# A matmul with a decayed cumulative sum: two PSUM banks for each of the first four tiles, weights loaded slot by slot, finer first pieces, and a last store in halves of time

## Chip, cores and metric

One core of one Trainium2 chip. The metric is the device time of the whole kernel in microseconds (us); several executions were timed and medians are quoted. The profiled execution has a span some 2 us shorter than its time, because the span begins with the first instruction.

## The reference

```python
# x (16, 2048, 1024), w (1024, 1024), decay (1024,), all float32
xw = x @ w
out[:, 0, :] = xw[:, 0, :]
for t in range(1, S):
    out[:, t, :] = decay[None, :] * out[:, t - 1, :] + xw[:, t, :]
```

## The kernel before

The 32768 rows of x are 64 chunks of 512 times. A **slot** is one output tile of 128 channels for a pair of chunks (1024 times, two PSUM banks, 16 matmuls), and the last two chunks make slots of one chunk each. For each chunk GpSimd issues loads that cast x to bf16, VectorE turns 32x32 blocks ("turn"), and ScalarE sorts the result into `xt` ("part"). TensorE leaves channels on partitions and time along the row. Then either VectorE scans PSUM directly, or, for "paired" tiles, ScalarE copies and scales (`pair`), GpSimd adds even to odd times, VectorE scans half as many elements with the squared decay, and GpSimd fills in the rest. VectorE turns the tile back, SyncE stores it. Every engine works in the order of a hand-written agenda.

```python
dec2 = psp.tile([128, 512], FP32, name="dec2")        # squared decay, has a PSUM bank to itself
...
def load_w(queue, h, e, m0=0, m1=M):                  # h: half of the columns, e: even/odd row, m: block
    for q in range(NQ):                               # four transfers of 32 partitions
        pin(queue.dma_start(
            out=stage[h, e, m0][quad(q)].rearrange("p (m d) -> p m d", m=m1 - m0),
            in_=_ap(w, [[2 * D, P], [2 * P * D, m1 - m0], [1, CH]],
                    (q * CQ + m0 * 2 * P + e) * D + h * CH)))
...
for _ in range(34):                                   # warming matmuls on zeros
    pin(nc.tensor.matmul(out=spare, lhsT=idle[:, 0:128], rhs=idle, start=True, stop=True))
load_w(nc.sync, 0, 0, 0, M // 2)                      # the others go out on GpSimd's queue
...
agenda = {                                            # M/L: x loads, U: w loads, W/w: w copy on VectorE/ScalarE,
    -99: "M0 M1 U0 U1 M2 M3 U2 U3 L L L W0 w1 E0 F0 G0 w3 W2 E1 F1 G1 W4 w5 W6 w7 E2 F2 D G2 E3 F3 G3 W8 W9 W10 W11",
    0: "w12 L L w13 P0 S0",                           # E/T: turn, F/G/X/Y: part, P: pair, S: scan,
    1: "w14 L P1 L",                                  # C: complete, B: turn back and store
    2: "S1 W15 P2 B0 S2",
    3: "T2 L S3 C0 C1 C2",
    4: "L P4 X2 L Y2 L B2 T3 B1 L",
    ...
    -1: "B-3 P-1 S-1 B-2 C-5 B-1 C-1 C-2",
}
...
heads = [ring(psp, "ps", 3, [128, T]) for _ in range(3)]     # three tiles with both banks
firsts = [ps[:, 0:TL] for ps in heads] + [spare]             # the fourth has one bank
# chunk 0 for four tiles, chunk 1 for three; the fourth's second half takes
# a bank of "ps" that the first scan has to free
...
for k in range(K):                                           # every later slot
    for l, c in enumerate(g):
        matmul(ps[:, l * TL:(l + 1) * TL], n, k, xt_of[c])
```

## Time and profile before

| | before |
|---|---|
| median of three executions | 915.26 us (915.03 to 915.39) |
| profiled span | 912.5 us |
| TensorE's first real matmul, from the start of the span | 11.20 us |
| TensorE's last matmul ends | 901.58 us |
| from there to the end (the "tail") | 10.9 us |

TensorE's work is fixed at 884 us, so only the beginning, the tail and waits between can be shortened. The prediction below shows the lines of the page, the timeline, the chain and the windows that say so. How to read them: in a timeline the first number is the start, the second the length, the brackets hold the idle time ahead and who ended it. In the chain of waits the first number is when a piece began and the second how long it lasted; for a DMA that is from issue to landing.

### The profile page before, as it was taken

Reading aid. Unit: us, or ns where it says so; the run is one execution under the profiler, and the core shown is the slowest. Engines: PE = TensorE matmul, PEld = TensorE weight load, DVE = VectorE, ACT = ScalarE, POOL = GpSimd, SP = SyncE. Lnnn points to the kernel's source line nnn. Section 1 sums busy time; section 2 is a strip of 40 time slices with the busy share of each in tenths; the row PEclk is TensorE's granted clock in tenths of the full one; section 3 lists DMA queues with packets and bytes.
Section 4 is the critical chain, followed back from the end, with each engine's and each line's share of the span. In section 5 each row is a group of like instructions: output and inputs, shape, how many; then the busy total and the mean of one; then the engine's idle time right before and its main releaser. Section 6 shows DMA issues by size and latency. Waiting matters only on the chain.

```text
span 912.5 us, 11926 instructions
## 1 busy us (share of the span) xinstructions
PE 891.3 (98%) x4088; PEld 408.5 (45%) x4170; DVE 826.0 (91%) x613; ACT 685.8 (75%) x950; POOL 664.4 (73%) x764
## 2 busy tenths in 40 slices
PE   8899999999999999999999999999999999999995
PEld 4444444444444444444444444444444444444442
DVE  4999999999999999999999999999999999999986
ACT  3778887877877777778778778778778778777753
POOL 8688878777777777777677777777787776776552
PEclk9999999999999999999999999999999999999998
DMA  9999999999999999999999999999999999999668
GB/s 170 166 220 215 215 230 235 256 250 255 247 237 255 247 237 224 230 233 231 223 235 227 224 231 229 230 226 231 227 224 230 231 230 224 232 229 207 151 151 219
DMA packets 406253, 204.49 MB, mean 224 GB/s; under 512 B 12976, under 2 KB 405936, under 8 KB 406192
## 3 DMA queue, kind: packets, MB, share of 16 engines
q1 hardware_dynamic: 268848, 134.76, 59.5%
q0 software_dynamic: 137344, 68.96, 56.8%
q8 instruction: 32, 0.52, 0.2%
q14 instruction: 29, 0.24, 0.1%
HBM read 138.42 MB, written 134.22 MB: 299 GB/s over the span
## 4 chain that ended last, share of the span: by engine, by line
PE 90%; DMA 3%; POOL 2%; issue 2%; DVE 2%; ACT 1%; SPq 0%; DVEq 0%; POOLq 0%
PE ps L126 90%; DMA xb<-in_x_dram 2%; POOL xb L105 1%; DMA ot<-in_w_dram 1%; DVE so L194 1%; DVE xw L115 1%; POOL ot L245 1%; PE spare L126 0%; DMA out_dram<-ot 0%; DVE so L180 0%; POOL so L208 0%; ACT xt L123 0%; DVE ot L215 0%; POOL xs L174 0%; ACT xs L168 0%
## 5 line engine op out<-in xcount | busy, mean ns | idle before, releaser
L126 PE MATMUL ps<-xt,wsb 128*128 128x512 bf16 (+1 forms) x4011 | 874.2, 377 | 9.0 <-DVE so L194 2.6
L126 PEld LDWEIGHTS <-wsb 128*128 128x128 bf16 x4136 | 404.6, 98 | 485.7 <-issue 5.6
L174 POOL TENSOR_TENSOR xs<-h,xs 128x512 f32<-128x512 f32 (+1 forms) x193 | 245.3, 1271 | 195.5 <-ACT h L158 88.3
L168 ACT COPY xs<-ps 128x1024 f32<-128x1024 f32 (+1 forms) x193 | 191.6, 993 | 158.8 <-PE ps L126 149.3
L215 DVE STREAM_TRANSPOSE ot<-so 128x1024 f32<-128x1024 f32 (+1 forms) x264 | 302.7, 1184 | 1.9 <-POOL so L208 1.1
L208 POOL TENSOR_TENSOR so<-h,xs 128x512 f32<-128x512 f32 (+1 forms) x193 | 244.3, 1266 | 34.5 <-ACT h L158 18.1
L123 ACT COPY xt<-xw 128x2048 bf16<-128x2048 bf16 (+1 forms) x128 | 239.8, 1875 | 7.5 <-DVE xw L115 7.5
L105 POOL DMA_DIRECT2D xb<-in_x_dram x264 | 174.1, 660 | 2.0 <-POOLq L435 0.9
L158 ACT ACTIVATE h<-so,dec 128x512 f32<-128x512 f32 (+1 forms) x193 | 147.1, 763 | 36.0 <-DVE so L180 32.1
L115 DVE STREAM_TRANSPOSE xw<-xb 128x2048 f32<-128x2048 f32 (+1 forms) x66 | 146.7, 2222 | 6.1 <-DMA xb<-in_x_dram 6.1
L180 DVE TENSOR_TENSOR_SCAN so<-dec,keep,xs 128x512 f32<-128x512 f32 (+1 forms) x99 | 121.6, 1229 | 29.8 <-POOL xs L174 29.6
L180 DVE TENSOR_TENSOR_SCAN so<-dec,xs 128x512 f32<-128x512 f32 x94 | 114.8, 1222 | 31.3 <-POOL xs L174 28.2
L158 ACT ACTIVATE h<-ps,dec 128x512 f32<-128x512 f32 (+1 forms) x193 | 131.8, 683 | 0.0
L194 DVE TENSOR_TENSOR_SCAN so<-dec,ps 128x1024 f32<-128x1024 f32 x33 | 74.5, 2261 | 0.0
L194 DVE TENSOR_TENSOR_SCAN so<-dec,keep,ps 128x1024 f32<-128x1024 f32 (+1 forms) x33 | 73.4, 2225 | 0.0
L211 ACT COPY keep<-so 128x1 f32<-128x1 f32 x136 | 25.1, 187 | 0.3 <-DVE so L194 0.3
L173 ACT COPY so<-keep 128x1 f32<-128x1 f32 x99 | 19.0, 192 | 0.7 <-DVE ot L215 0.7
L171 POOL MEMSET so<- 128x1 f32 x94 | 11.0, 117 | 3.2 <-DVE ot L215 3.2
L262 PE MATMUL spare<-idle 128*128 128x512 bf16 x34 | 10.2, 473 | 1.2 <-DVE idle L259 1.2
L126 PE MATMUL spare<-xt,wsb 128*128 128x512 bf16 (+1 forms) x43 | 11.2, 359 | 0.1
L245 POOL DMA_DIRECT2D ot<-in_w_dram x16 | 9.0, 561 | 2.4 <-issue 0.7
L253 ACT COPY wsb<-ot 128x512 bf16<-128x512 bf16 x6 | 3.4, 615 | 5.7 <-DMA ot<-in_w_dram 5.7
(18 smaller groups left out, 20.3 us busy)
## 6 DMA issues: line engine op xcount, KB each, us to landing
out_dram<-ot SPq DMA_DIRECT2D x248, 512.0 KB, 10.6
xb<-in_x_dram POOLq DMA_DIRECT2D x248, 256.0 KB, 7.8
out_dram<-ot SPq DMA_DIRECT2D x12, 256.0 KB, 4.2
xb<-in_x_dram POOLq DMA_DIRECT2D x16, 128.0 KB, 5.0
ot<-in_w_dram POOLq DMA_DIRECT2D x12, 128.0 KB, 5.2
out_dram<-ot SPq DMA_DIRECT2D x8, 128.0 KB, 2.8
ot<-in_w_dram SPq DMA_DIRECT2D x4, 128.0 KB, 3.5
ot<-in_w_dram POOLq DMA_DIRECT2D x4, 64.0 KB, 4.3
```

Of the source, the lines that this page charges most:

```text
L105: pin(nc.gpsimd.dma_start(out=xb_of[c][quad(q), j0:j1], in_=_ap(x, [[D, P], [P * D, j1 - j0], [1, CQ]], (b * S + t0 + j0 * P) * D + q * CQ)))
L115: pin(nc.vector.transpose(out=dst.rearrange("p (m j i) -> p j m i", m=M, i=P)[:, j0:j1], in_=src.rearrange("p (j m c) -> p j m c", m=M, c=P)))
L123: pin(copy(out=xt_of[c][:, m0:m1, :, j0 * P:j1 * P], in_=src))
L126: pin(nc.tensor.matmul(out=ps[:, t0:t1], lhsT=wsb[:, k, n].rearrange("p q i -> p (q i)"), rhs=xt[:, k // 2, k % 2, t0:t1], start=(k == 0 a ...
L158: pin(nc.scalar.activation(out=h, in_=src, func=mybir.ActivationFunctionType.Copy, scale=dec[:, self.n:self.n + 1]))
L168: pin(nc.scalar.copy(out=self.xs, in_=self.ps))
L174: pin(nc.gpsimd.tensor_tensor(out=self.xs[:, 1:T:2], in0=g, in1=self.xs[:, 1:T:2], op=ALU.add))
L180: pin(nc.vector.tensor_tensor_scan(out=so[:, 3:T + 2:2], data0=dec2[:, n:n + 1].to_broadcast([128, T // 2]), data1=self.xs[:, 1:T:2], init ...
L194: pin(nc.vector.tensor_tensor_scan(out=so[:, t:t + size], data0=dec[:, n:n + 1].to_broadcast([128, size]), data1=ps, initial=before, op0=A ...
L208: pin(nc.gpsimd.tensor_tensor(out=so[:, 2:T + 2:2], in0=h, in1=self.xs[:, 0:T:2], op=ALU.add))
L211: pin(nc.scalar.copy(out=self.keep, in_=so[:, T + 1:T + 2]))
L215: pin(nc.vector.transpose(out=self.ot[:, :, n % R * P:(n % R + 1) * P], in_=self.so[:, 2:T + 2].rearrange("p (i t) -> p i t", t=P)))
```

## The change

The intent: the squared decay gives up its PSUM bank, so that all four first tiles have two banks and none waits for a scan. Each weight transfer now holds one (half, parity, block) for all 128 partitions, so that each copy needs one landing instead of four, in the order in which they are used. The first turns and parts are cut finer and the warming is shorter, so that real work can start earlier. At the end the last two tiles are turned and stored in two halves of time.

```diff
-    dec2 = psp.tile([128, 512], FP32, name="dec2")
+    squares = [const.tile([128, K], FP32, name="squares")]   # a PSUM bank after slot 7 ("d")
...
-    def load_w(queue, h, e, m0=0, m1=M):
-        for q in range(NQ):
-            pin(queue.dma_start(
-                out=stage[h, e, m0][quad(q)].rearrange("p (m d) -> p m d", m=m1 - m0),
-                in_=_ap(w, [[2 * D, P], [2 * P * D, m1 - m0], [1, CH]],
-                        (q * CQ + m0 * 2 * P + e) * D + h * CH)))
+    def load_w(queue, i):
+        h, e, m = i // 8, i // 4 % 2, i % 4
+        m0 = M // 2 if (h, e) == (0, 0) and m >= M // 2 else 0
+        pin(queue.dma_start(
+            out=stage[h, e, m0][:, (m - m0) * CH:(m - m0 + 1) * CH],
+            in_=_ap(w, [[CQ * D, NQ], [2 * D, P], [1, CH]], (m * 2 * P + e) * D + h * CH)))
...
+    pin(nc.scalar.copy(out=idle[:, 0:1], in_=idle[:, 1:2]))  # the warming has to wait for it
-    for _ in range(34):
+    for _ in range(27):
...
-    load_w(nc.sync, 0, 0, 0, M // 2)
+    load_w(nc.sync, 0)
+    load_w(nc.sync, 1)
...
-        -99: "M0 M1 U0 U1 M2 M3 U2 U3 L L L W0 w1 E0 F0 G0 w3 W2 E1 F1 G1 ...
-        0: "w12 L L w13 P0 S0",
-        1: "w14 L P1 L",
-        2: "S1 W15 P2 B0 S2",
+        -99: "M0 M1 U2 U3 U4 U5 U6 U7 M2 M3 U8 ... U13 w1 U14 L U15 W0 L L L E0 F0 G1 E1 L F2 G3 ...
+        0: "L P0",
+        1: "w13 w14 S0",
+        2: "L P1 P2 S1 L S2 w12 B0",
... (slots 3 to 16 sorted anew)
-        -1: "B-3 P-1 S-1 B-2 C-5 B-1 C-1 C-2",
+        -1: "B-3 P-1 S-1 a-2 C-5 a-1 C-1 C-2 b-2 b-1",     # a, b: first and second half of time
...
-            firsts = [ps[:, 0:TL] for ps in heads] + [spare]
+            firsts = [ps[:, 0:TL] for ps in heads] + [spares[0]]
+            seconds = [ps[:, TL:T] for ps in heads] + [spares[1]]
...
+        if left == 2 - R:                                      # buffers of the last two tiles
+            outlets = [Outlet(range(n, K), nj // 2, i) for i in range(2)]
...
+            if step == K:                                      # slot 8: all of its first chunk, then the second
+                todo.sort(key=lambda kl: kl[1])
```

## The prediction

> **What bounds the kernel now.** I read the page first (busy shares), then the timeline of TensorE, then the chain that ended last, then the windows of the last 30 us. The page says which engine, the timeline says where that engine is not at work.
>
> ```profile
> span 912.5 us, 11926 instructions
> PE 891.3 (98%) x4088; PEld 408.5 (45%) x4170; DVE 826.0 (91%) x613; ACT 685.8 (75%) x950; POOL 664.4 (73%) x764
> ...
> L126 PE MATMUL ps<-xt,wsb 128*128 128x512 bf16 (+1 forms) x4011 | 874.2, 377 | 9.0 <-DVE so L194 2.6
> ```
>
> TensorE is busy for 98% of the span. The work is fixed: 32768 rows are 64 chunks of 512, each chunk takes 8 output tiles x 8 contractions, so 4096 matmuls of 512 columns, before and after. The 377 ns is the pipelined length of one, not its rate; the rate comes from the timeline, where the long pieces of the chain repeat every 10.79 us for 50 matmuls, 0.2158 us each. 4096 x 0.2158 = 884 us. So at most 912.5 - 884 = 28.5 us of the span is open to any change that leaves the matmuls alone. Where it lies:
>
> ```profile
> 1.20 10.17 PE L262 MATMUL spare<-idle 128*128 128x512 bf16 x34 [1.20 <-DVE idle L259]
> 11.20 0.49 PE L126 MATMUL ps<-xt,wsb 128*128 128x256 bf16 x3
> ...
> 13.01 0.50 PE L126 MATMUL ps<-xt,wsb 128*128 128x256 bf16 x3 [0.77 <-DVE wsb L253]
> ...
> 14.89 0.49 PE L126 MATMUL ps<-xt,wsb 128*128 128x256 bf16 x3 [0.83 <-DVE xt L123]
> ...
> 20.64 5.70 PE L126 MATMUL ps<-xt,wsb 128*128 128x256 bf16 x48 [0.39 <-DVE xt L123]
> 27.59 1.89 PE L126 MATMUL ps<-xt,wsb 128*128 128x512 bf16 x7 [1.25 <-DVE so L194]
> 29.77 7.07 PE L126 MATMUL ps<-xt,wsb 128*128 128x512 bf16 x32 [0.29 <-DVE so L194]
> 37.69 27.79 PE L126 MATMUL ps<-xt,wsb 128*128 128x512 bf16 x125 [0.86 <-DVE so L194]
> 65.71 4.48 PE L126 MATMUL ps<-xt,wsb 128*128 128x512 bf16 x20 [0.23 <-DVE so L194]
> ```
>
> First number: start; second: length; in brackets the idle time before and who ended it. Real work starts at 11.20, right behind 34 warming matmuls on zeros. By 37.69 the first six slots (96 matmuls, 20.7 us) are done: 37.69 - 11.20 - 20.7 = 5.8 us idle, in two kinds: early on it waits for weights and input pieces, from 26 to 38 us for a scan to free a PSUM bank. From 37.69 on 4000 matmuls x 0.2158 = 863.2 us would end at 900.9; they end at 901.6. So the middle is full. The tail from 901.6 to 912.5 is 10.9 us. Sum: 11.2 + 5.8 + 0.7 + 10.9 = 28.6.
>
> ```profile
> 24.38 8.03 DMA xb<-in_x_dram
> ...
> 38.70 2.28 DVE xw L115
> ...
> 42.81 1.89 ACT xt L123
> ```
>
> In the chain, the beginning is loads: the issue and landing times in the trace show the transfers landing in order, 256 KB of source every 0.65 us (about 400 GB/s), with never more than eight in flight. Chunk 3 has landed at 37.8, is turned until 41.0 and copied until 44.7, and slot 8, the first that needs it, starts at about 44.6.
>
> ```profile
> 902.00:903.00 1.00, 0.00 (x0) 0.00 (x0) 1.00 (x2) 0.00 (x0) 0.26 (x1) 1.00 0.94 238
> ...
> 908.00:909.00 1.00, 0.00 (x0) 0.00 (x0) 0.00 (x0) 0.00 (x0) 0.00 (x0) 0.50 0.92 198
> ```
>
> After TensorE's last matmul the windows show the DMA engines at 0.92 to 0.94 (last but one column) up to 911. The queue of stores has been without a gap since 895: the last twelve issues follow each other at 0.6 to 1.1 us, the last at 908.66 lands at 911.30. VectorE's last transpose is done at 905.55, 3 us before that issue. The tail is stores that drain, not VectorE.
>
> **What the Trainium skill says.** "TensorE: Matmul & The Clock Gate", section "Wait — 56ns, not 53.3ns?", gives 215.7 ns from start to start for 512 columns warm; the trace has 215.8, so the floor stands. "PSUM — Partial Sum Buffer", section "Terms", says that one matmul output is at most one bank of eight: before, three pairs of banks plus one spare bank plus one bank that only held the squared decay; head 3 of the beginning had no second bank, and its second half had to wait for a scan, which is the 1.25 us wait above. "DMA: Bandwidth & Descriptors", section "Why a DMA increments its semaphore by 16 and not by 1", says that a transfer spreads over the largest number up to 16 that divides the slowest dimensions of both sides. The old weight loads have 32 on both sides, so 16 engines; the new ones have 128 in the buffer and 4 in memory, so 4 engines. No transfer of that form is in this trace; this is my main risk. The same page, section "Rules for kernel authors", says that under 64 KB one pays mostly overhead; the new half stores are 64 KB each.
>
> **The change part by part.**
> Warming: 27 instead of 34 matmuls, 7 x 0.213 = 1.5 us less; they end at about 9.7.
>
> First piece: x half 0 landed at 8.48. Before, a turn of 1.25 and a copy of 1.05 stood before the first matmul. VectorE's turns of 1024 and 2048 elements took 1.25 and 2.29, so a quarter of 512 takes about 0.21 + 0.52 = 0.73; a copy of one m 0.37 on VectorE and 0.62 on ScalarE (by the same line through 1.05 and 1.90). So 8.60 + 0.73 + 0.37 = 9.7, and TensorE starts at 9.8: **1.4 us earlier**.
>
> Weights by slot: the same 4 MB in 16 transfers instead of 20, each usable alone. With one landing per 0.65 us after 11.20, the six transfers for the first half land from 11.9 to 15.3, x of chunk 1 from 15.9 to 20.5 (before 16.2 to 21.2), the second half of w until 27.1, chunk 2 until 31.1, chunk 3 until 36.4 (before 37.8).
>
> Four heads: TensorE then does chunk 0 by 19.0 (20.3 before; the wait for half 1 of x at 11.2 stays, 1.8 us), starts chunk 1 at 19.2 and finishes all four heads at about 26.3, instead of three at 26.3 and the fourth at 29.3. Slot 4 takes the banks of head 0, free when VectorE's first scan ends: VectorE has copied its last weights at 24.4, the scan takes 2.27, 26.65. Then a new wait: the weight piece for slot 4's second contraction is copied on ScalarE behind slot 2's two copies (25.7 + 0.9 + 0.7 + 0.6), ready at 27.9. So slot 4 runs from about 27.9 less two matmuls, 2.3 us earlier than 29.77, and then four slots x 3.45 bring slot 8 to **41.4** against 44.6.
>
> Slot 8: chunk 3 landed at 36.4; VectorE reaches its turn at 38.0 (scans, one turn, three transposes queued before it), done 40.2; ScalarE has two tiles' copies first, so the two pieces are ready at 42.5 and 44.3. The change sorts slot 8 by chunk, so they are needed at 43.1 and 44.0: a wait of 0.3. After it: slot 10 wants the scan of slot 7 (VectorE free at 48.0, TensorE there at 48.6), slot 11 wants ScalarE's copies of slot 8 (51.6 against 52.0). Close, both met. So 3.0 us remain gained when the full stretch begins, and its 0.2 and 0.2 us of waits before 65.7 stay.
>
> Squares: a tiny multiplication, once in SBUF and once into the freed bank; 0.17 us on VectorE, nothing.
>
> Tail: VectorE's two last transposes become four of half the length, the first half's data is complete some 0.5 us sooner. But the store queue is then still issuing older stores. Four issues of 128 KB at 0.62 become eight of 64 KB; at the same bytes per us 8 x 0.31, at the 0.25 to 0.38 of the smallest issues in the trace (the decay loads) up to 8 x 0.35. The second halves go into a buffer whose stores must have landed first (before: 906.55), later than VectorE is ready, but no later than the queue is. Net 0, with 0.4 either way.
>
> Sum: 1.4 (start) + 1.6 (fewer idle us until slot 8) = 3.0, less 0.3 for a quarter to a third of a risk that the new weight loads cost 1 us: 2.8. 915.26 - 2.8 = **912.4**.
>
> **Rivals.**
> (a) The weight loads run on four engines each. The first two, from the sync queue, would both sit on the same four and make the x pieces late there; w pieces would land near 6 and 9 instead of 6.5 at the latest, x half 0 after 9.5. For it: the page's rule and the shape. Against it: consecutive transfers may rotate over engines, and the author cut the warming to 27, which fits a start at 9.7. It would cost 1 to 1.5 us at the start and some of the later landings: 913.5 to 915.
> (b) The gain at the beginning is given back because VectorE, nearly without idle time from 25 to 65 us in the trace, has the same work to do in less time, and a scan holds up slot 10 to 14 (as the wait of 0.23 at 65.71 shows already). For it: total VectorE work rises slightly (quarters have fixed costs). Against it: the order of the transposes is changed so that scans come first. It would leave 1 to 1.5 us: 914.
> (c) The loads bind less than I think and slot 8 can start at 40: 911. Against it: landings at 400 GB/s.
> (d) The tail gains because the last piece is smaller, or loses by issue cost: 0.5 us either way.
>
> **Range and chances.** 909.8 to 915.0 covers (a) to (d) singly and half of (c) with (d); the runs before spread by 0.36. Faster by over 2% would take 18.3 us of the 28.5 that are open, while start and tail keep some 20: 1%. Slower by over 2% needs a new standing wait in the middle, whose code is unchanged: 1%.
>
> **What would show it.** TensorE's first real matmul at 9.8 (not 11.2); no wait for a scan of 1.25 us before the last head; slot 4 near 27.5 and slot 8 near 41.4; TensorE idle 4 us instead of 5.8 before that, some of it before slot 4 on a weight copy; then full to the end near 898.6; a tail of 10.9 us with the DMA engines above 0.9. The prediction fails if the weight transfers land later than the pieces before, or if waits for scans of over 1 us appear between 45 and 70 us.

## The result, and the profile after

**The kernel became slower: 925.51 us (925.00 to 926.06, five executions) against 915.26 (913.81 to 915.55, five executions).** The ratio is 1.0115, with a 95% interval of 1.010 to 1.013. Ratios here and below are the mean time of one kernel's runs over that of the other's of the same rounds, so not quite the ratio of the medians. The chances favoured "within 2%", which came true, but 925.5 lies far outside the range of 909.8 to 915.0, and the sign was wrong.

The page after, the same three lines as before:

```profile
span 923.5 us, 11920 instructions
...
PE 894.2 (97%) x4081; PEld 408.6 (44%) x4163; DVE 829.2 (90%) x623; ACT 687.4 (74%) x956; POOL 665.6 (72%) x762
...
L126 PE MATMUL ps<-xt,wsb 128*128 128x512 bf16 (+1 forms) x3996 | 877.0, 379 | 15.4 <-DVE xt L123 6.2
```

Waits ahead of the matmuls grew from 9.0 to 15.4 us, the largest part is for input (`xt`). Where they lie, in TensorE's timeline of the first 75 us:

```profile
2.29 8.04 PE L275 MATMUL spare<-idle 128*128 128x512 bf16 x27 [2.29 <-ACT idle L273]
15.04 0.80 PE L126 MATMUL ps<-xt,wsb 128*128 128x256 bf16 x3 [4.71 <-DVE xt L123]
...
19.84 1.44 PE L126 MATMUL ps<-xt,wsb 128*128 128x512 bf16 x3 [0.70 <-DVE xt L123]
...
31.29 2.34 PE L126 MATMUL ps<-xt,wsb 128*128 128x256 bf16 x20 [0.38 <-DVE xt L123]
...
36.39 0.38 PE L126 MATMUL ps<-xt,wsb 128*128 128x512 bf16 x1 [1.88 <-DVE so L194]
39.88 35.41 PE L126 MATMUL ps<-xt,wsb 128*128 128x512 bf16 x150 [3.11 <-ACT wsb L265]
```

Warming ends at 10.3 and real work starts at 15.04, not at the predicted 9.8. Three matmuls of 256 columns take 0.80 us where they took 0.49 before: the clock is at half speed. Slot 4 loses 1.88 us to a scan and 3.11 us to the copy of a weight piece, and starts in earnest at 39.88 instead of 29.77. From there TensorE is full. It ends at 912.07, 10.5 us later than before, and the tail is 11.4 us, 0.5 longer: 10.5 + 0.5 = 11.0, the difference of the spans.

What the first matmul waited for is in the chain:

```profile
2.60 10.91 DMA xb<-in_x_dram
...
15.23 7.18 DMA ot<-in_w_dram
...
27.33 9.34 DMA ot<-in_w_dram
36.69 1.14 ACT wsb L265 x2
...
39.32 0.52 ACT wsb L265
```

The third piece of x, issued at 2.60 as before, took 10.9 us to land; before, issued at the same moment, it took 5.2. The code of the x loads is unchanged. From 15 us on the chain is weights, which TensorE finally waits for at 39.88. The windows from 12 to 18 us, before and then after, show the same (the last two columns are the DMA engines' mean share and GB/s, the one before them the clock):

```profile
12.00:18.00 6.00, 4.35 (x33) 3.02 (x32) 2.67 (x5) 2.80 (x4) 5.78 (x11) 1.00 1.30 186
```

```profile
12.00:18.00 6.00, 2.60 (x12) 1.67 (x12) 3.30 (x6) 2.47 (x4) 4.85 (x7) 0.61 0.70 85
```

Loads move at 85 instead of 186 GB/s, and the sixteen DMA engines are busy half as much on the mean (this share adds up packets that overlap, so it can exceed 1), while transfers are outstanding. The queue of DMA issues lists the median from issue to landing: 5.0 us for the first x pieces before, 6.7 after, and 5.2 against 7.1 for the weights of 128 KB.

| landed at, us | before | after |
|---|---|---|
| chunk 0, first half | 8.48 | 13.69 |
| last weight piece | 27.07 | 38.97 |
| chunk 3 (slot 8 needs it) | 37.77 | 48.22 |

Everything that the beginning needs comes 5 to 12 us later. In the tail, the windows show stores still draining, as before:

```profile
915.00:920.00 5.00, 0.00 (x0) 0.00 (x0) 1.28 (x4) 0.00 (x0) 0.00 (x0) 0.50 0.98 201
```

### The profile page after: what moved, and what is told of

The parts are those of the page before. It is cut to its first block, busy times and chain, and to the rows that moved or that the text cites. A ratio compares the mean times of both kernels' runs of the same rounds, so it can differ in the third digit from the quotient of the medians.

```text
span 923.5 us, 11920 instructions
## 1 busy us (share of the span) xinstructions
PE 894.2 (97%) x4081; PEld 408.6 (44%) x4163; DVE 829.2 (90%) x623; ACT 687.4 (74%) x956; POOL 665.6 (72%) x762
## 4 chain that ended last, share of the span: by engine, by line
PE 93%; DMA 3%; POOL 1%; issue 1%; ACT 0%; DVE 0%; SPq 0%; DVEq 0%; POOLq 0%
PE ps L126 93%; DMA ot<-in_w_dram 2%; DMA xb<-in_x_dram 1%; POOL ot L258 1%; DMA out_dram<-ot 0%; PE spare L126 0%; POOL xb L105 0%; DVE ot L219 0%; SPq L240 0%; ACT wsb L265 0%; ACT xs L167 0%; DVE so L194 0%; ACT h L157 0%; DVE so L179 0%; POOL xs L173 0%
## 5 line engine op out<-in xcount | busy, mean ns | idle before, releaser
L126 PE MATMUL ps<-xt,wsb 128*128 128x512 bf16 (+1 forms) x3996 | 877.0, 379 | 15.4 <-DVE xt L123 6.2
L219 DVE STREAM_TRANSPOSE ot<-so 128x1024 f32<-128x1024 f32 (+2 forms) x266 | 302.7, 1176 | 2.0 <-issue 1.2
L179 DVE TENSOR_TENSOR_SCAN so<-spare,keep,xs 128x512 f32<-128x512 f32 (+1 forms) x99 | 121.7, 1230 | 30.5 <-POOL xs L173 30.2
L179 DVE TENSOR_TENSOR_SCAN so<-spare,xs 128x512 f32<-128x512 f32 x90 | 110.0, 1222 | 30.7 <-POOL xs L173 27.7
L126 PE MATMUL spare<-xt,wsb 128*128 128x512 bf16 (+1 forms) x58 | 14.3, 361 | 0.2 <-issue 0.2
L170 POOL MEMSET so<- 128x1 f32 x94 | 10.9, 116 | 0.4 <-DVE ot L219 0.4
L275 PE MATMUL spare<-idle 128*128 128x512 bf16 x27 | 8.0, 470 | 2.3 <-ACT idle L273 2.3
```

Of the source, the lines that this page charges most:

```text
L126: pin(nc.tensor.matmul(out=ps[:, t0:t1], lhsT=wsb[:, k, n].rearrange("p q i -> p (q i)"), rhs=xt[:, k // 2, k % 2, t0:t1], start=(k == 0 a ...
L179: pin(nc.vector.tensor_tensor_scan(out=so[:, 3:T + 2:2], data0=squares[-1][:, n:n + 1].to_broadcast([128, T // 2]), data1=self.xs[:, 1:T:2 ...
L219: pin(nc.vector.transpose(out=outlet.ot[:, :, c0:c0 + P], in_=self.so[:, 2 + t0:2 + t0 + nj * P].rearrange("p (i t) -> p i t", t=P)))
```

## The experiments

The theory after the result (A): the new weight transfers are slow because of their shape, they hold up the x loads as well, and nearly the whole loss is theirs. Rivals: (B) the new order of work on ScalarE and VectorE, above all the weight copy put behind two pairs; (C) TensorE's clock, cold after a long wait; (D) the tail; (E) the squared decay in SBUF. Twelve kernels were run. "Before" is the kernel before on the same chip and in the same rounds, whose medians were 914.85 to 915.27.

**1. The change with the old weight loads.** Only `load_w` and its calls go back; heads, order, parts, squares and tail stay.

```diff
-        "U": lambda i: load_w(nc.gpsimd, i),
+        "U": lambda i: load_w(nc.gpsimd, *{2: (0, 0, M // 2, M), 4: (0, 1), 8: (1, 0), 12: (1, 1)}[i]),
-        -99: "M0 M1 U2 U3 U4 U5 U6 U7 M2 M3 U8 U9 U10 U11 U12 U13 w1 U14 L U15 ...
+        -99: "M0 M1 U2 U4 M2 M3 U8 U12 w1 L ...        # and load_w as before
```

> The changed kernel with the weight loads of the kernel before (20 transfers with 32 as the slowest dimension on both sides), everything else as changed. Theory A (the cause is the shape of the new weight loads, which run on few DMA engines): x half 0 lands near 8.5 us again, the first real matmul is at 9.8 to 10.3, no cold stretch of the clock before the end, slot 4 at 27 to 29; time 911 to 914.5. Rival B (the quarters, the new order of the copies and the banks are at fault): first matmul after 12, a wait of some 3 us before slot 4's second contraction stays, time 920 or more.

Measured: 916.38 us (914.42 to 918.00), ratio 1.0011 (0.9995 to 1.0027), no difference clear of noise to before. Chunk 0's half landed at 8.66, the last weight at 27.74, chunk 3 at 38.45. The profiled execution was the slowest of the four (918.0). Its timeline:

```profile
10.16 0.49 PE L126 MATMUL ps<-xt,wsb 128*128 128x256 bf16 x3
...
25.25 0.60 PE L126 MATMUL ps<-xt,wsb 128*128 128x256 bf16 x4 [1.54 <-DVE xt L123]
26.33 3.89 PE L126 MATMUL ps<-xt,wsb 128*128 128x256 bf16 x20 [0.48 <-DVE xt L123]
...
32.42 24.06 PE L126 MATMUL ps<-xt,wsb 128*128 128x512 bf16 x108 [0.99 <-ACT wsb L265]
```

So 925.51 - 916.38 = 9.1 us of the loss go with the old loads, and TensorE starts at 10.16. But the 2.8 us that I had expected to gain do not come either: this version is level with the kernel before.

**2. The kernel before with the new weight loads.** The converse.

```diff
-    load_w(nc.sync, 0, 0, 0, M // 2)
+    load_w(nc.sync, 0)
+    load_w(nc.sync, 1)
-        load_w(nc.gpsimd, *((0, 0, M // 2, M), (0, 1), (1, 0), (1, 1))[i])
+        for s in ((2, 3), (4, 5, 6, 7), (8, 9, 10, 11), (12, 13, 14, 15))[i]:
+            load_w(nc.gpsimd, s)                        # and load_w as after
```

> The kernel before with only the weight loads replaced by the new ones (one transfer for each slot, 128 partitions against 4 as the slowest dimension in memory). Theory A: x half 0 lands at 12 to 14 us, first real matmul after 14, the last weight piece after 36, time 921 to 926. Rival B: within 1 us of the kernel before.

Measured: 926.23 us (925.48 to 927.05), ratio 1.0122 (1.0106 to 1.0139), as slow as the whole change. Chunk 0's half landed at 13.40, the last weight at 37.47, chunk 3 at 48.31. In its timeline the first real work and the wait that comes last are

```profile
15.55 0.80 PE L126 MATMUL ps<-xt,wsb 128*128 128x256 bf16 x3 [4.09 <-DVE xt L123]
...
47.79 12.39 PE L126 MATMUL ps<-xt,wsb 128*128 128x512 bf16 x48 [2.48 <-DVE so L194]
```

The loads alone reproduce the loss. It doesn't need the new order (B), nor the tail (D), nor the squares (E).

**3. Only the order of dimensions on the memory side.** What in the new loads is slow: 128 partitions, size, number, or the small outer dimension of the source? Here the kernel before keeps its twenty transfers, 32 partitions each, and the same bytes; only the source now names the blocks (2 or 4 of them) first and the 32 rows second. The elements therefore arrive in the wrong places and the result is wrong.

```diff
-                in_=_ap(w, [[2 * D, P], [2 * P * D, m1 - m0], [1, CH]],
-                        (q * CQ + m0 * 2 * P + e) * D + h * CH)))
+                in_=_ap(w, [[CQ * D, m1 - m0], [2 * D, P], [1, CH]],
+                        (q * 2 * P + e) * D + h * CH)))
```

> The kernel before with its own 20 weight transfers, same bytes, same 32 partitions, same row length, same issue order; only the order of the dimensions on the memory side is changed, so that the slowest one there is 2 (the 8 small transfers) or 4 (the other 12). It fetches wrong rows, so its result is wrong on purpose. If the number of DMA engines follows the slowest dimensions (theory A in its narrow form): the loads land late as in the changed kernel or later, x half 0 after 11 us, time 920 to 930. Rival C (it is the 128 partitions of the buffer, or the larger transfers, not the slowest dimension): x half 0 lands at 8.5, time within 1.5 us of the kernel before.

Measured: 930.02 us (929.61 to 931.20), ratio 1.0163 (1.0148 to 1.0178). Chunk 0's half landed at 15.00, the last weight at 42.89.

```profile
22.60 0.80 PE L126 MATMUL ps<-xt,wsb 128*128 128x256 bf16 x3 [11.99 <-DVE xt L123]
```

The four loads on the sync queue land at 6.88, 11.54, 15.50 and 19.84 here, and VectorE, which works in order, copies them before it turns x: hence the start at 22.60.

Neither the 128 partitions nor the fewer, larger transfers are needed for the harm: the order of the source's dimensions is enough. This is what the rule that the prediction quoted (engines by the slowest dimensions of both sides: 32 and 2 or 4) asks for. The same edit also changes how source rows are paired with destination rows, which a wrong result can't separate from the count of engines. But the packed traces can: they keep each update that the DMA side makes to a transfer's semaphore, of which `prof` shows only the last.

| | before | the change | experiment 3 |
|---|---|---|---|
| slowest dimension in memory, sync-queue weights | 32 | 4 | 2 |
| updates for one such load | 16 | 1 early, 4 late | 1 early, 2 late |
| x, third piece, 16 updates | all by 7.77 | 12 by 7.87, 4 at 12.67 to 13.51 | 14 by 7.31, 2 at 12.15 to 12.77 |

So the x piece was complete at the old time but for four parts in sixteen (two in experiment 3), as many as the dimension says, and these came only when the second sync load was through (its four updates: 11.45 to 12.55 in the change). The x loads are held up on the few engines that the sync-queue weights use. For the loads on GpSimd's queue, which show 16 updates in either form, the count can't be read off in this way.

**4. The copy for slot 4 ahead of the pairs.** The change, with ScalarE's copy of weight piece 12 moved up. This tests (B) at the place of the 3.11 us wait.

```diff
-        1: "w13 w14 S0",
-        2: "L P1 P2 S1 L S2 w12 B0",
+        1: "w12 w13 w14 S0",
+        2: "L P1 P2 S1 L S2 B0",
```

> The changed kernel with one copy moved: ScalarE's copy of the weight piece of slot 4's second contraction goes ahead of the two others and of slot 2's copies. If its place in ScalarE's order costs the 3.1 us wait at 39.88 and the cold stretch of 6.8 us behind it (9 matmuls at 0.43 instead of 0.216), the second matmul of slot 4 comes at 36.7 to 37.5 and the time falls by 2.5 to 4.5 us against the changed kernel, to 921 to 923. If the late loads bind anyway (chunk 3 of x, landed at 48.2, is needed at slot 8), it falls by less than 1.

Measured: 925.24 us (924.02 to 925.77), ratio 1.0107 (1.0092 to 1.0122). The wait of 3.11 us is gone (0.67 at 40.49 is left), yet only 0.3 us is gained. Slot 8 now waits for chunk 3, which lands at 48.95, by 1.67 us at 55.11 and 0.78 at 56.91. A wait that the profile shows as the largest was worth almost nothing, because the next late load stood behind it.

**5. The order made for the old loads.** Experiment 1 with the copies sorted so that nothing stands before slot 4: this asks why its gain is missing.

```diff
-        ... G13 W8 F12 E7 F14 L G15 D W9 W10 W11",
+        ... G13 F12 E7 F14 L G15 D W8 W9 W10 W11",
-        1: "w13 w14 S0",
-        2: "L P1 P2 S1 L S2 w12 B0",
-        3: "L C0 w15 C1 C2 T2",
+        1: "w12 w13 w14 S0",
+        2: "L P1 P2 S1 W15 L S2 B0",
+        3: "L C0 C1 C2 T2",
```

> The first experiment (the changed kernel with the old weight loads) with three copies moved to suit loads that arrive in fours: the copy of slot 4's first weight piece goes behind the last input copies of chunk 1, the one of its second contraction ahead of slot 2's copies, the one of its last contraction back to VectorE. Theory: the first experiment missed 912 only because its order of copies was made for pieces that arrive one by one (waits of 1.54, 0.48 and 0.99 us at 25 to 32 us and a cold stretch from 26.9 to 30.3). Then TensorE does chunk 1 without the 1.54 us wait, slot 4 comes at 28 to 29, and the time is 911.5 to 914. Rival: the waits move elsewhere (slot 8 on chunk 3, or scans), and it stays at 914.5 to 917.

Measured: 917.35 us (915.16 to 917.71), ratio 1.0021 (1.0008 to 1.0035): slower than before, if only by 0.2%. TensorE's timeline and a window of it:

```profile
28.17 15.76 PE L126 MATMUL ps<-xt,wsb 128*128 128x512 bf16 x70 [0.60 <-DVE so L194]
45.60 1.02 PE L126 MATMUL ps<-xt,wsb 128*128 128x512 bf16 x4 [1.67 <-ACT xt L123]
47.40 27.87 PE L126 MATMUL ps<-xt,wsb 128*128 128x512 bf16 x120 [0.78 <-ACT xt L123]
```

```profile
48.00:50.00 2.00, 2.00 (x6) 0.68 (x5) 2.00 (x3) 0.90 (x5) 1.92 (x1) 0.50 1.04 128
```

Slot 4 starts at 28.17, close to the predicted 27.5 to 27.9. But slot 8 waits for ScalarE's parts of chunk 3, and VectorE's timeline says why:

```profile
36.59 1.18 DVE L194 TENSOR_TENSOR_SCAN so<-dec,spare 128x512 f32<-128x512 f32 x1
37.88 1.28 DVE L194 TENSOR_TENSOR_SCAN so<-dec,so,spare 128x512 f32<-128x512 f32 x1
39.08 2.35 DVE L219 STREAM_TRANSPOSE ot<-so 128x1024 f32<-128x1024 f32 x2
41.34 2.27 DVE L115 STREAM_TRANSPOSE xw<-xb 128x2048 f32<-128x2048 f32 x1
```

Chunk 3 has landed at 38.16 but is turned only from 41.34, behind two scans and two turns back that leave no idle time. After the two waits the clock stands at half speed from 46.8 to 50.2 (0.50 in the window), which costs another 1.7 us. The start gained is given back at slot 8.

**6 and 7. One group of the new loads at a time.** Experiment 6 is the change with only the two sync-queue loads (0 and 1) old, experiment 7 with only these two new.

```diff
-    load_w(nc.sync, 0)                                     # experiment 6
-    load_w(nc.sync, 1)
+    load_w_old(nc.sync, 0, 0, 0, M // 2)
```

```diff
-        "U": lambda i: load_w(nc.gpsimd, i),               # experiment 7
+        "U": lambda i: load_w_old(nc.gpsimd, *{2: (0, 0, M // 2, M), 4: (0, 1), 8: (1, 0), 12: (1, 1)}[i]),
```

> The changed kernel with the old shape for the first two weight pieces alone, those from the sync queue; the 14 others stay new. Theory A: input half 0 lands at 8.5 to 9 us and the first real matmul is at 10 to 10.5, but the later weight pieces still land slowly (the last after 30 us), so chunk 3 lands at 42 to 45 and the time is 918 to 922. If the first two alone were the cause, the time is under 916.5.

> The reverse: the changed kernel with the new shape for the first two weight pieces alone, the 14 others in the old shape. Theory A: input half 0 lands at 12.5 to 13.7 and the first real matmul comes at 14 to 15, cold; after it the loads go at the old pace, so that chunk 3 lands at 41 to 43 and the time is 918 to 922, the two losses adding up to about that of the changed kernel.

Measured: 920.88 us (919.13 to 921.58), ratio 1.0062, and 920.92 us (920.49 to 921.48), ratio 1.0066. Against the 916.4 of experiment 1 each group costs 4.5 us, and 4.5 + 4.5 is the 9.1 of both. They act at different times: with the first two old, chunk 0's half lands at 8.29 but the last weight at 34.90; with only these two new, at 13.20 and 32.79. So two transfers issued at 0.75 and 1.52 us put off the x pieces of another queue by 4.5 us (13.20 against 8.66 in experiment 1). The later fourteen put off weights and chunks 2 and 3.

**8. The new tail alone.** The kernel before, with the last two tiles turned and stored in halves, in the same buffers as after the change.

```diff
-        -1: "B-3 P-1 S-1 B-2 C-5 B-1 C-1 C-2",
+        -1: "B-3 P-1 S-1 a-2 C-5 a-1 C-1 C-2 b-2 b-1",     # and back() with two half buffers
```

> The kernel before with only the tail changed: the last two slots transposed and stored by halves of time, the second half into the buffer whose stores have to land first. From the traces, the time from TensorE's end to the end was 10.9 us before and 11.4 to 11.5 with the new tail: 0.3 to 0.7 us slower than the kernel before. The prediction had 0 with 0.4 either way. If it gained as intended, 0.3 to 0.5 faster.

Measured: 915.74 us (914.89 to 916.41, five rounds) against 914.85, ratio 1.0008 (0.9994 to 1.0022): unclear by the times alone. Its tail is 11.66 us. VectorE's last instruction, before, and then in this run:

```profile
904.28 1.27 DVE L215 STREAM_TRANSPOSE ot<-so 128x512 f32<-128x512 f32 x2
```

```profile
907.54 0.77 DVE L220 STREAM_TRANSPOSE ot<-so 128x256 f32<-128x256 f32 x2 [1.64 <-DMA out_dram<-ot]
```

The second halves wait for the stores of the buffer that they reuse. That wait isn't the loss, though: the turn ends at 908.31, while the first store of a second half is issued only at 909.91, right behind those of the first halves. What grew are the issues: the last four of 128 KB took 2.45 us before (906.75 to 909.20), the eight of 64 KB take 4.12 here (907.70 to 911.82); that each of these lands sooner (2.3 us after its issue in the change, the median, against 2.8 before) gives part of it back. The tails of all traces together say more than the times: eight kernels with the new tail have 11.1 to 11.7 us, mean 11.4 (the change and experiments 1, 4 to 8 and 10); six with the old one have 10.4 to 10.9, mean 10.6 (before and experiments 2, 3, 9, 11, 12). The two ranges do not overlap, so the halves cost about 0.8 us.

**9. A candidate.** Old loads, old tail, four heads, and slots 2 to 7 sorted anew so that chunk 3 is turned as soon as it has landed. Extract:

```diff
-        4: "P4 S3 X2 B2 B1 L T3 Y2",
-        5: "S4 C3 L",
-        7: "S7 L C5 X4 S6 C6 B7 d B5",
+        4: "P4 C2 S3 X2 L T3",
+        5: "P5 C3 Y2 y3 B2 S4 L",
+        7: "S7 B1 T4 S5 L C5 X4 S6 C6 B7 d B5",
```

> Old weight loads, old tail, four heads with a bank each, quarters at the beginning, and VectorE's and ScalarE's orders at slots 2 to 7 rearranged: chunk 3's turn as soon as it has landed, half of its copy on VectorE, the scan of slot 7 before the turn of chunk 4. The reordered first experiment stood at slot 8 for 1.67 and 0.78 us on chunk 3, and a half-clock stretch of 3.4 us followed. If these are gone, slot 8 comes at 42 without a wait and without the stretch; TensorE ends at 899.5 to 901 and the time is 912 to 914.5. If VectorE, with the same work in less time, now holds up slots 9 to 14 with scans, the waits move there and the time is 914.5 to 917.

Measured: 929.08 us (928.15 to 929.73), ratio 1.0149. Slot 8 did start at 41.9 without a wait, but TensorE then stood for 15.23 us at 67.8. The fault was mine: slot 1's turn back, put off to slot 7, keeps a buffer that GpSimd needs, GpSimd was blocked from 36.7 to 48.95, and chunk 4's loads stood behind it in GpSimd's order.

**10. Longer warming.** The change with 50 warming matmuls instead of 27, for (C).

```diff
-    for _ in range(27):
+    for _ in range(50):
```

> The changed kernel with 50 instead of 27 warming matmuls, so that TensorE is busy until the first input has landed and the clock stays at full speed from the beginning. If the cold stretch from 13 to 23.5 us is a part of the loss: TensorE does chunk 0 some 3 us sooner, and the time falls by 1 to 3 us. If the loads bind whatever TensorE does (last weight pieces at 36.7, chunk 3 at 48): chunk 1 still waits for its input at 25 to 28, and the time changes by less than 0.7 us.

Measured: 924.38 us (923.84 to 924.80), ratio 1.0099 (1.0085 to 1.0113), 1.1 us less than the change. The clock was at full speed until 37.8. The change runs at half speed from 13.3 to 23.5, which by itself looks like a loss of over 3 us of matmul time. Most of it is not on the path: chunk 3 lands at 47.60 here, and what TensorE saves early it waits later.

**11. The squares in SBUF.** The kernel before, with the squared decay moved out of PSUM, for (E). After the change four early scans read it from SBUF.

```diff
-    dec2 = psp.tile([128, 512], FP32, name="dec2")
+    dec2 = const.tile([128, K], FP32, name="dec2")
```

> The kernel before with the squared decay in SBUF for the whole run, not in a PSUM bank, which the change does for its first scans. In the changed kernel the scans that read it from SBUF took 1.88 and 2.00 us twice, where they took 1.22 otherwise, each time until an addition on GpSimd ended; in the kernel before no such scan is over 1.5 us. If reading both operands from SBUF makes a scan wait for GpSimd's addition, the mean of the 193 scans grows from 1.22 to 1.5 or more, VectorE (826 us busy) becomes the bound and the time is over 930. If those two were chance, within 1 us.

Measured: 920.62 us (918.74 to 921.48), ratio 1.0056 (1.0042 to 1.0069). I had expected a larger loss, over 930; the direction was right. The group of scans without a kept value, before, after the change (four scans only), and in this run:

```profile
L180 DVE TENSOR_TENSOR_SCAN so<-dec,xs 128x512 f32<-128x512 f32 x94 | 114.8, 1222 | 31.3 <-POOL xs L174 28.2
```

```profile
L179 DVE TENSOR_TENSOR_SCAN so<-squares,xs 128x512 f32<-128x512 f32 x4 | 6.3, 1573 | 2.5 <-POOL xs L173 2.5
```

```profile
L180 DVE TENSOR_TENSOR_SCAN so<-dec,xs 128x512 f32<-128x512 f32 x94 | 154.5, 1643 | 2.2 <-POOL xs L174 2.2
```

One scan takes 1643 ns instead of 1222 when both of its operands lie in SBUF, and GpSimd's additions are hardly longer (mean 1316 and 1276 ns instead of 1271 and 1266). The packed trace shows when they are long: 110 of this run's 193 scans took over 1.4 us (none did before), each of them began while an addition ran on GpSimd, and each ended 1.08 to 1.09 us after that addition. In the change two of the four took 1.88 and 2.00 us and ended 1.08 and 1.09 us after such an addition (not with it, as I had written in the expectation), so the bank that was taken from the squares cost the change about 4 x 0.35 = 1.4 us of VectorE's time at the beginning, which the prediction had put at nothing. What of this reaches TensorE was not measured alone. In experiment 11 most of the loss is in one place: TensorE waits 2.99 us for a scan until 69.93, and the clock is at half speed from 69.68 to 73.10.

**12. The candidate mended.** Experiment 9 with slot 1's turn back earlier, chunk 4's loads ahead of it and the squares in PSUM from slot 4 on.

```diff
-        4: "P4 C2 S3 X2 L T3",
-        5: "P5 C3 Y2 y3 B2 S4 L",
-        7: "S7 B1 T4 S5 L C5 X4 S6 C6 B7 d B5",
-        8: "B4 L B6 P8 C7",
+        4: "P4 C2 S3 d X2 L L T3",
+        5: "P5 C3 Y2 y3 B1 B2 S4",
+        7: "S7 L B4 S5 S6",
+        8: "P8 C5 C6 C7 B5 T4 B7 L B6",
```

> The candidate again with its own fault mended: in it the transpose of slot 1's result was put so late that GpSimd, which writes into that buffer next, stood still for 12 us with the loads of chunk 4 queued behind it, and TensorE for 15. Slot 8 itself came at 41.9 without a wait, as wanted. Now that transpose goes ahead, the loads of chunk 4 go ahead of it on GpSimd, the scans of slots 7, 5 and 6 before the turn of chunk 4, and the squares go into the PSUM bank as soon as it is free. If nothing else blocks: slot 8 at 41.9 without a wait, no wait over 1 us after it, TensorE's end at 899.5 to 901.5, time 911.5 to 914 (0.2 to 0.4% faster than the kernel before). If VectorE's work before slot 14 binds whatever the order: waits for scans at slots 10 to 14 of 2 us and more, 914.5 or later.

Measured: 916.95 us (916.82 to 918.08, five rounds), ratio 1.0021 (1.0008 to 1.0035). TensorE's timeline and then ScalarE's:

```profile
28.43 31.51 PE L126 MATMUL ps<-xt,wsb 128*128 128x512 bf16 x144 [0.51 <-DVE so L194]
63.86 11.39 PE L126 MATMUL ps<-xt,wsb 128*128 128x512 bf16 x45 [3.92 <-ACT h L157]
```

```profile
58.15 1.90 ACT L123 COPY xt<-xw 128x2048 bf16<-128x2048 bf16 x1 [1.79 <-DVE xw L115]
61.56 0.75 ACT L157 ACTIVATE h<-so,dec 128x512 f32<-128x512 f32 x1 [1.52 <-DVE so L179]
62.23 0.99 ACT L167 COPY xs<-ps 128x1024 f32<-128x1024 f32 x1
63.12 0.69 ACT L157 ACTIVATE h<-ps,dec 128x512 f32<-128x512 f32 x1
```

From 28.43 there is no wait at slot 8 (reached near 42) and none until about 60. Then slot 13 waits 3.92 us for slot 10's bank, which ScalarE empties only at 63.8, because it waited twice for VectorE (1.79 and 1.52 us). Before that, VectorE had itself waited 0.79 and 1.11 us for GpSimd (until 50.10 and 54.67), and ScalarE 3.38 us for it (until 50.10), so VectorE's work alone doesn't explain this wait. A half-clock stretch of 3.4 us follows. Three us are gained at slot 8 and more than that is lost at slot 13. No version beats the kernel before.

## Why the prediction was wrong

**The step that failed: "With one landing per 0.65 us after 11.20".** The new weight transfers do not land at the old rate. In the second half of w they landed 0.3 to 2.1 us apart, 1.25 on the mean (29.50 to 36.98 for seven; ahead of the eighth, at 38.97, a piece of x lands), where the old ones came 0.71 apart for the same bytes (22.08 to 27.07 for eight), and the first two of them put x off by 4.5 us, because they ran on few engines and the x pieces had to share these (the table in experiment 3). The prediction named this as rival (a), "my main risk", and then sized it at 1 to 1.5 us and put 0.3 us of it into the sum. It was 9.1 us (experiment 1 takes it away, 2 brings it alone, 6 and 7 split it into halves). The two reasons against it were weak: that the author had cut the warming to 27 says what the author hoped, not when loads land; and that consecutive transfers may rotate over engines was an assumption without a line behind it; the two sync loads were done one after the other (at 6.56 and 12.55; the rival had 6 and 9), and each x piece from the second to the eighth was late in four parts, not eight. One place was left out of the sizing: GpSimd's issues wait for earlier landings (never more than eight in flight), so one late load puts off the issue of the eighth after it. The second weight load on that queue went out at 12.28, after x's second piece had landed at 11.99, instead of at 7.33; the fourth at 14.45 instead of 8.76.

**The rest of the sum failed too, though smaller: "So 3.0 us remain gained when the full stretch begins".** With the old loads the start is as predicted: first real matmul at 9.86 to 10.16 (predicted 9.8), slot 4 at 28.2 (predicted 27.5 to 27.9) once the copies are sorted for it, slot 8 near 42 (predicted 41.4) in experiment 12. The warming itself ends at 10.33 in the change, not at 9.7: the working overlooked the ScalarE copy ahead of it, which puts its start from 1.20 to 2.29. One term failed even with the old loads: chunk 3 was to land at 36.4, 1.4 us before its old time, though the bytes ahead of it are the same. It landed at 38.45 and 38.16 (experiments 1 and 5; 37.77 before), and the wait at slot 8, put at 0.3, was 1.67 and 0.78 in experiment 5. But experiments 1, 5 and 12 end 1.1 to 2.5 us above the kernel before (the 1.1 us of experiment 1 within its uncertainty). Rival (b) was right in kind: in experiment 5 VectorE is busy all the time from 45 to 65 us, and what TensorE gained came back as waits for ScalarE, which waited for VectorE. That VectorE's work leaves no room whatever the order is argued and not shown: in experiment 12 GpSimd held up VectorE and ScalarE as well, and only three orders were tried with the old loads besides the change's own. The rival was undersized ("would leave 1 to 1.5 us"), for two reasons that the runs show. Idle gaps of TensorE of 2 us and more in all can be followed by a stretch of 3.4 us at half clock, so that 2.5 us of waiting cost 4.2. And the squares in SBUF make VectorE's early scans longer.

**Four heads** did remove the wait of the fourth tile for a scan, as predicted: TensorE goes through all four heads without it in the change. The scan for slot 4 then cost 1.88 us there, since it waited for late data.

**The weight copy ahead of slot 4**, predicted as a small new wait until 27.9, became 3.11 us. It was the largest wait in the timeline but not the cause: moving the copy up brought 0.3 us (experiment 4).

**The tail** was predicted at 0 with 0.4 either way. It lost 0.5 us in this pair of traces and 0.8 us over fourteen. The term that was mis-sized is the eight issues of 64 KB: 4.1 us, 8 x 0.51 (experiment 8), where I had taken 8 x 0.31 to 8 x 0.35. The wait of the second halves for their buffer is there (1.24 us ahead of the last turn in the change) but hidden behind the store queue, as argued: that turn ends at 917.52, and the first store of a second half goes out at 919.13. (The queue "without a gap" before has a gap of 0.4 us, at 903.66.)

**Right:** the floor and TensorE's rate, that a 2% change either way was out of reach, and that the tail is stores that drain.

What stays open: whether some order of work keeps the gain; how many engines the new loads on GpSimd's queue used, which was read only for the sync queue; and the exact condition for the half clock, since 2.48 us brought it and a single wait of 2.28 us, earlier in the same trace (experiment 2), did not.

## What to carry to other kernels

Before regrouping loads, look at the slowest dimension on both sides of each transfer; a tidy transfer of 128 partitions with a source that starts with a dimension of 4 landed at little more than half the rate here (one per 1.25 us instead of 0.71) and held up loads of other queues. When a trace holds no transfer of a new form, a rule of a page is evidence and belongs into the sum at full size until a run says otherwise. A gain at the beginning has to be followed by the engines behind the bound one; here, in the orders tried, they didn't. And the largest wait in a timeline can be worth no more than the distance to the next one (0.3 us of 3.11 in experiment 4).

## What the Trainium skill lacked or had wrong

- "DMA: Bandwidth & Descriptors", section "Why a DMA increments its semaphore by 16 and not by 1": its rule predicts which loads were slow, and the runs agree (930.0 against 915.2 us when only the order of the source's dimensions changes). That section gives no figure for what few engines cost, nor for what they do to transfers of other queues: two such loads moved the landing of x on another queue from 8.66 (experiment 1) to 13.20 us (experiment 7).
- "TensorE: Matmul & The Clock Gate", section "Why this matters for your kernels", asks for no idle gaps over about 3 us. Here shorter gaps were followed by half clock: one of 2.48 us (experiment 2), and 1.67 with 0.78 soon after (experiment 5), while single ones of 1.81 (experiment 12) and 2.28 us (experiment 2) were not, nor 1.67 with 0.78 in experiment 4. Each stretch before the tail lasted 3.4 us or a multiple of it, which agrees with the window of 3413 ns in the page's section "What's actually happening".
- "SBUF — State Buffer", section "SBUF: two separate sides", has the lock between a VectorE operation with two SBUF inputs and GpSimd, and the runs agree: 1643 against 1222 ns for one scan on the mean, and the long scans are those that began during an addition (experiment 11). It gives no figure for what keeping the broadcast operand in PSUM is worth in a kernel: 5.4 us here (920.6 against 915.3).
